# Ordering edges behind the side work of a hybrid S5/HGRN2 block, S5 parameters made in the first feed-forward part, the S5 scan placed in the heads, and ring quarters exchanged

## The chip, the cores and the metric

One core of one Trainium2 chip runs the kernel in one launch. The metric is device time in microseconds. Five engines work beside each other, each with its own in-order queue: TensorE (PE, with its weight loads PEld), VectorE (DVE), ScalarE (ACT), GpSimd (POOL), and SyncE (SP), which here issues nearly all DMAs.

## The reference, cut to what matters

All data is float32, 1024 tokens of width 1024.

```
h = x
h += 0.5 * swiglu(rmsnorm(h), gate, up, down)          # ffn1, hidden width 2816
u = rmsnorm(h);  s5_in, q, f, i, g, ga, gb = split(u @ w_in)
y_s5 = S5 scan of s5_in: states x_t = lam_bar * x_(t-1) + B_bar u_t (32 groups x 64 complex
       states), y = Re(C x) + D u;   lam_bar = exp(lam * dt), from the parameters alone
y_a  = (gelu(y_s5) @ glu_val) * sigmoid(gelu(y_s5) @ glu_gate)
o    = HGRN2 over 8 heads of 128 (gated linear recurrence), head norm, * silu(g)
h += (sigmoid(ga) * y_a + sigmoid(gb) * (o @ hg_w_out)) @ w_merge_out
h += 0.5 * swiglu(rmsnorm(h), ...)                     # ffn2
h += sigmoid(rmsnorm(h) @ ple_gate) * (p @ ple_proj);  out = rmsnorm(h)
```

## The kernel before, in words

Every large product is made on PE from pairs of rounded float32 parts: an operand is split by `split` or `piece` into hi (an ACT copy, L330 or L98) and lo (a subtraction on DVE or POOL, L331 or L99), and `mm3` issues three matmuls for each pair (L339). Weights come by DMA (L80) into two raw buffers and are split into 7 slots of a ring; a slot is refilled as soon as a product gives it back.

**FFN.** Hidden blocks f = 0 to 3 (`plain`) are multiplied directly, blocks 4 to 21 (`strassen`) by seven products of quarter size, of some 19 us for a block. The seven operands of the token side (A11, A22, A12 and the sums S1 to S4, made by `operands`) lie in seven "quarters" q0 to q6 of SBUF, four of which hold the normed input itself until block 3 is done. While blocks 5 to 21 run, 15 "jobs" prepare the down product: each loads 1 MB of the down weights (L578; the last four load x instead, L583) into a room of `r1`, makes four differences on DVE (L587) and stores them to DRAM (L600). The activations go to DRAM too (`gave`, L501). The down product (L707) then reads both back through rings in q4 and q5 (L612, L620) and splits each block on the way (`ready`).

**Side work.** Two lists, `queue` and `scan`, hold functions and waits. `tick` is called every few matmuls of the main products; it takes one element of each list: an integer n is a wait of n ticks, a function traces its instructions. `flush` and `scanned` empty a list at once. The framework orders the instructions of each engine itself: one that is traced later can be put ahead of one traced earlier, if the framework's planner holds it ready first.

**Mixer.** After the S5 input product (4 units) come the gates gg, ga, gb in `pair` form (again seven products, which begin with `flush("a11")`), then the eight HGRN2 heads (`hg_q`, `hg_f`, `hg_v`, with `hg_steps` in `queue`: seven levels of matmuls L1179, masked copies L1185 and multiplications L1191, L1192, then `kt`, `state`, `outp`, `back`), the S5 output product (glu), and the merge. `refill`, in the last gb pair, brings the normed input back into q0 for the heads. The S5 work is in `scan` from the first gg pair on: `lower_bound` and `s5_params` (225 small DVE instructions, L736 to L862, and two Sin on ACT, L812), then `s5_mats` for 8 blocks, then two turns of the scan proper (`turn`), each of 29 calls of `madd` with eight DVE instructions (L990 to L997), with matmuls and copies around them. A turn is 115 ticks long by its list. The scan works in `r1`; heads that end before it does spill their output (L1278).

Of the kernel before, what the change touches and what calls it, by code (L numbers as in the profile page):

```python
# [11 lines left out]
P = 128  # L12
# [38 lines left out]
class Weights:  # L51
# [23 lines left out]
    def fetch(self):  # L75
        while self.fetched < len(self.items) and len(self.items[self.fetched][1]) <= self.raw_free:
# [135 lines left out]
class Block:  # L212
# [58 lines left out]
    def tick(self):  # L271

        for q in (self.queue, self.scan):
# [144 lines left out]
    def operands(self, gain, roles=(0, 1, 2, 3, 4, 5, 6)):  # L418
# [18 lines left out]
        def sums(k):  # L437
# [3 lines left out]
            self.split(self.quarter(S1, k), s1, g)  # L441
# [5 lines left out]
        def plain(q, j, h):  # L447
            self.split(self.quarter(q, j % 4), scaled(j, h), (v, g)[j % 2])

# [7 lines left out]
        def chain(work, gap=0):  # L457
# [5 lines left out]
            sums=chain(sums, 4 if gain else 0),  # L463
# [21 lines left out]
    def ffn(self, name, gain, source, each, late=None):  # L485
# [30 lines left out]
        def plain(f):  # L516
            for h in range(2):
# [55 lines left out]
        def jobs():  # L573

            def load(n):
                room = self.r1[:, 4 * (n % 4):4 * (n % 4) + 4, :]
# [24 lines left out]
            begin(0)  # L601
            begin(1)
            for n in range(NP + 4):
                yield [lambda n=n: begin(n + 2), 2] + [x for i in range(4) for x in (lambda n=n, i=i: work(n, i), 3)] + [
                    lambda n=n: end(n)]
# [75 lines left out]
        ops = self.operands(gain)  # L681
# [19 lines left out]
        for n, (i, p) in enumerate(steps):  # L701
# [9 lines left out]
            for s in parts.pop(n):  # L711
                w.give(s)
            if n + 4 > len(steps):
                w.limit = None
# [38 lines left out]
    def lower_bound(self, p):  # L753
# [6 lines left out]
        nc.sync.dma_start(out=raw, in_=self.io["hg_lower_bound"])  # L760
        m = p.tile([P, HEADS], F32, name="lbm")
# [8 lines left out]
        v.tensor_scalar(out=self.lb1, in0=self.lb, scalar1=-1.0, scalar2=1.0, op0=ALU.mult, op1=ALU.add)  # L770

# [12 lines left out]

    def s5_params(self, pool):
# [8 lines left out]
        nc.sync.dma_start(out=a, in_=io["s5_log_dt"])  # L794
        self.sgn = c.tile([P, 1], F32, name="sgn")
        v.memset(self.sgn, 1.0)
        v.memset(self.sgn[64:128, :], -1.0)
        self.exp_small(pool, dt, a, SH, "s5x")
        er, sn, cs = (tl("s5" + n) for n in ("er", "sn", "cs"))
        v.tensor_tensor(out=a, in0=lre, in1=dt, op=ALU.mult)  # L800
        self.exp_small(pool, er, a, SH, "s5y")
        v.tensor_tensor(out=a, in0=lim, in1=dt, op=ALU.mult)
# [11 lines left out]
        self.pwr = pool.tile([P, G, T5 + 1], F32, name="s5pwr")  # L814
        self.pwi = pool.tile([P, G, T5 + 1], F32, name="s5pwi")
# [9 lines left out]
        self.rvr = pool.tile([P, G, T5], F32, name="s5rvr")  # L825
        self.rvi = pool.tile([P, G, T5], F32, name="s5rvi")
# [3 lines left out]
        yield  # L830

        wr, wi = tl("s5wr"), tl("s5wi")
# [13 lines left out]
        v.tensor_tensor(out=d, in0=d, in1=sc, op=ALU.mult)  # L846
        v.tensor_tensor(out=a, in0=a, in1=d, op=ALU.mult)
# [4 lines left out]
        self.wr = wr  # L852
        self.wis = tl("s5wis")
        v.tensor_scalar(out=self.wis, in0=wi, scalar1=self.sgn[:, 0:1], scalar2=None, op0=ALU.mult)

        self.chr = c.tile([P, 9, G // 2], F32, name="chr")
        self.chi = c.tile([P, 9, G // 2], F32, name="chi")
        for dst, src in ((self.chr, self.pre[T5]), (self.chi, self.pim[T5])):
# [3 lines left out]
        for i in range(2, 9):  # L862
            k, m = i // 2, i - i // 2
            self.cmul(pool, self.chr[:, i, :], self.chi[:, i, :], self.chr[:, k, :], self.chi[:, k, :],
                      self.chr[:, m, :], self.chi[:, m, :], [P, G // 2])
        self.d5 = c.tile([GH, G], F32, name="d5")
        nc.sync.dma_start(out=self.d5, in_=io["s5_d"])
        self.qd = self.dram.tile([8, P, 4, P], F32, name="s5q")
        self.pd = self.dram.tile([8, P, 4, P], F32, name="s5p")
        self.kd = self.dram.tile([GH, G, P], F32, name="s5k")  # L870
# [70 lines left out]
    def s5_steps(self):  # L941
# [12 lines left out]
        r4 = xr.rearrange("p g (a i) -> p g a i", i=NS)  # L954
        i4 = xi.rearrange("p g (a i) -> p g a i", i=NS)
        xs = pool.tile([P, RG, NCH], F32)
        u2 = pool.tile([P, RG, NCH], F32)
        prod = [pool.tile([P, GP * SC], F32) for _ in range(4)]
# [4 lines left out]
        steps = [lambda: self.lower_bound(early), 8]  # L963
        params = self.s5_params(early)
# [15 lines left out]
        def madd(dre, dim, sre, sim, lre, lim, shape):  # L980

            n = 1
# [3 lines left out]
            def view(x):  # L986
                x = x[:, 0:n]
                return x if len(shape) == 2 else x.rearrange("p (a b) -> p a b", b=shape[2])
            p1, p2, p3, p4 = (view(x) for x in prod)
            v.tensor_tensor(out=p1, in0=sre, in1=lre, op=ALU.mult)  # L990
            v.tensor_tensor(out=p2, in0=sim, in1=lim, op=ALU.mult)
            v.tensor_tensor(out=p3, in0=sim, in1=lre, op=ALU.mult)
            v.tensor_tensor(out=p4, in0=sre, in1=lim, op=ALU.mult)
            v.tensor_tensor(out=dre, in0=dre, in1=p1, op=ALU.add)
            v.tensor_tensor(out=dre, in0=dre, in1=p2, op=ALU.subtract)
            v.tensor_tensor(out=dim, in0=dim, in1=p3, op=ALU.add)
            v.tensor_tensor(out=dim, in0=dim, in1=p4, op=ALU.add)  # L997

        def turn(r):
# [35 lines left out]
            def local(i):  # L1035
                s = [P, GP, SC]
                bc = lambda x: x[:, 1, gp].unsqueeze(2).broadcast_to(s)
                madd(r4[:, :, :, i], i4[:, :, :, i], r4[:, :, :, i - 1], i4[:, :, :, i - 1],
                     bc(self.chr), bc(self.chi), s)
            for i in range(1, NS):  # L1040
                steps += [lambda i=i: local(i), 2]

            def carry(a0, a1):
                for a in range(a0, a1):
                    madd(r4[:, :, a, NS - 1], i4[:, :, a, NS - 1], r4[:, :, a - 1, NS - 1], i4[:, :, a - 1, NS - 1],
                         self.chr[:, NS, gp], self.chi[:, NS, gp], [P, GP])
            for a in range(1, SC, 2):
                steps += [lambda a=a: carry(a, min(SC, a + 2)), 2]

            def spread(i):  # L1050
                s = [P, GP, SC - 1]
# [715 lines left out]
```

## Time and profile before

| | |
|---|---|
| median of 3 runs | 2626.4 us (2623.2 to 2634.38) |
| the profiled execution, its own time | 2635.56 us |
| its span, first to last instruction | 2633.7 us |
| busy: PE, DVE, ACT, POOL | 2472.1, 1893.4, 914.0, 864.3 us |
| mean granted TensorE clock | 0.968 of full |

An engine's idle time is 2633.7 less its busy time. The granted clock is 1 at 2.4 GHz and 0.5 at 1.2 GHz; a stretch with a mean of 0.9 spent a fifth of its time at the lower level.

### The profile page before, as it was taken

The numbers are of one execution on the slowest core, as the hardware profiler recorded it, in microseconds if no ns is written. First come the engines' busy times: TensorE is split into PE (matmuls) and PEld (weight loads), VectorE is DVE, ScalarE is ACT, GpSimd is POOL, SyncE is SP. The second block draws the span as 40 slices with busy tenths as digits, with TensorE's granted clock in tenths as the row PEclk, the third lists the DMA queues.
The fourth block names the chain that finished last, engine by engine and source line by source line (L and its number), as shares of the span: only waits on it lengthen the run. The fifth ranks groups of instructions, "written<-read, shape, count | busy, mean of one in ns | idle before, by whom it ended". The sixth has DMA issues, their size and how long they took to land. (4 is left out here: it accounts for less than half of the span.)

```text
span 2633.7 us, 34224 instructions
## 1 busy us (share of the span) xinstructions
PE 2472.1 (94%) x12030; PEld 2067.5 (79%) x12030; DVE 1893.4 (72%) x3302; ACT 914.0 (35%) x1592; POOL 864.3 (33%) x602
## 2 busy tenths in 40 slices
PE   9999999999988998898999998989999999899997
PEld 7777778788866776787898887868877788688886
DVE  8898666658899678649545666946898766657756
ACT  4322232445443343231322223323322323345532
POOL 3254445100234544120211124552354444300143
PEclk9999999999998998899999999999999999899998
DMA  3478433867322345150231224452378432676313
GB/s 133 150 245 275 161 97 120 280 200 239 110 75 79 121 158 150 30 120 25 66 93 41 73 88 140 128 164 81 119 259 276 162 118 86 229 252 193 126 57 105
DMA packets 193932, 370.03 MB, mean 140 GB/s; under 512 B 34752, under 2 KB 49344, under 8 KB 193728
## 3 DMA queue, kind: packets, MB, share of 16 engines
q1 hardware_dynamic: 193072, 367.30, 42.7%
q8 instruction: 95, 1.56, 0.3%
q14 instruction: 77, 0.63, 0.1%
q10 hardware_dynamic: 688, 0.55, 0.1%
HBM read 255.84 MB, written 111.94 MB: 140 GB/s over the span
## 5 line engine op out<-in xcount | busy, mean ns | idle before, releaser
L339 PE MATMUL mm<-q,wsplit 128*128 128x512 f32 (+1 forms) x7452 | 1721.0, 391 | 89.0 <-ACT q L330 46.5
L339 PEld LDWEIGHTS mm<-q,wsplit 128*128 128x128 f32 x7452 | 1387.7, 191 | 390.8 <-ACT q L330 53.3
L99 POOL TENSOR_TENSOR wsplit<-wraw,wsplit 128x512 fp32r<-128x512 f32 x368 | 526.9, 1445 | 1162.6 <-ACT wsplit L98 470.8
L98 ACT ACTIVATE wsplit<-wraw 128x512 fp32r<-128x512 f32 x464 | 283.9, 625 | 520.4 <-DVE wraw L119 196.1
L707 PE MATMUL mm<-wsplit 128*128 128x512 f32 x1848 | 426.5, 394 | 14.7 <-ACT wsplit L330 13.7
L707 PEld LDWEIGHTS mm<-wsplit 128*128 128x128 f32 x1848 | 350.7, 190 | 90.2 <-ACT wsplit L330 14.5
L331 DVE TENSOR_TENSOR wsplit<-space,wsplit 128x512 fp32r<-128x512 f32 x308 | 208.4, 714 | 126.1 <-PE mm L707 93.3
L330 ACT ACTIVATE wsplit<-space 128x512 fp32r<-128x512 f32 x308 | 193.1, 631 | 212.4 <-PE mm L707 175.2
L119 DVE TENSOR_TENSOR wraw<-wraw 128x512 f32<-128x512 f32 x153 | 174.2, 1138 | 69.2 <-POOL wsplit L99 63.3
L99 POOL TENSOR_TENSOR wsplit<-t,wsplit 128x512 fp32r<-128x512 f32 x51 | 85.6, 1678 | 266.6 <-ACT wsplit L98 232.0
L534 DVE TENSOR_TENSOR t<-t,mm 128x512 f32<-128x512 f32 x252 | 166.2, 677 | 0.2
L1179 PE MATMUL mm<-space,space 128*128 128x128 f32 x896 | 114.1, 282 | 25.2 <-DVE space L1139 14.9
L1179 PEld LDWEIGHTS mm<-space,space 128*128 128x128 f32 x896 | 109.8, 197 | 31.3 <-DVE space L1139 15.8
L99 DVE TENSOR_TENSOR wsplit<-wraw,wsplit 128x512 fp32r<-128x512 f32 x96 | 85.3, 891 | 66.1 <-ACT wsplit L98 60.5
L1185 DVE COPY_PREDICATED space<-masks,mm 128x256 f32<-128x256 int32 x112 | 58.4, 521 | 90.6 <-PE mm L1179 90.5
L587 DVE TENSOR_TENSOR r<-r 128x512 f32<-128x512 f32 x120 | 104.5, 882 | 13.0 <-DMA r<-in_ffn_w_down_dram 6.1
L339 PE MATMUL mm<-wsplit,q 128*128 128x256 f32 x768 | 101.5, 288 | 0.0
L339 PEld LDWEIGHTS mm<-wsplit,q 128*128 128x128 f32 x768 | 95.2, 193 | 0.5 <-PE mm L1244 0.4
L98 ACT ACTIVATE wsplit<-t 128x512 fp32r<-128x512 f32 x51 | 32.3, 633 | 174.9 <-DVE t L119 156.7
L505 POOL TENSOR_TENSOR a<-a 128x512 f32<-128x512 f32 x44 | 66.4, 1508 | 64.9 <-DVE a L525 48.3
L1308 DVE TENSOR_TENSOR t<-t,mm 128x512 f32<-128x512 f32 x105 | 69.5, 677 | 19.2 <-ACT t L1311 9.3
L537 ACT ACTIVATE t<-t 128x512 f32<-128x512 f32 x72 | 45.5, 631 | 104.5 <-DVE t L534 104.5
(247 smaller groups left out, 2120.2 us busy)
## 6 DMA issues: line engine op xcount, KB each, us to landing
space<-ffn_act SPq DMA_DIRECT2D x154, 256.0 KB, 3.5
ffn_act<-a SPq DMA_DIRECT2D x110, 256.0 KB, 3.7
wraw<-in_ffn_w_gate_dram SPq DMA_DIRECT2D x44, 512.0 KB, 3.4
wraw<-in_ffn_w_up_dram SPq DMA_DIRECT2D x44, 512.0 KB, 5.0
r<-in_ffn_w_down_dram SPq DMA_DIRECT2D x22, 1024.0 KB, 6.4
ffn_sums<-r SPq DMA_DIRECT2D x22, 1024.0 KB, 8.8
wraw<-in_w_in_dram SPq DMA_DIRECT2D x44, 512.0 KB, 3.5
space<-ffn_sums SPq DMA_DIRECT2D x88, 256.0 KB, 2.7
```

The costliest lines, as they stand in the source:

```text
L98: self.nc.scalar.activation(hi, src, AF.Copy)
L99: engine.tensor_tensor(out=lo, in0=src, in1=hi.bitcast(F32), op=ALU.subtract)
L119: sub = lambda out, x, y: v.tensor_tensor(out=out, in0=x, in1=y, op=ALU.subtract)
L330: self.nc.scalar.activation(hi, src, AF.Copy)
L331: lo_engine.tensor_tensor(out=lo, in0=src, in1=hi.bitcast(F32), op=ALU.subtract)
L339: self.last = nc.tensor.matmul(ps, al if p == 2 else ah, bl if p == 1 else bh, start=p == order[0] and i == 0, stop=p == order[2] and i == ...
L505: g.tensor_tensor(out=x[n], in0=x[a], in1=x[b], op=op)
L534: add = lambda out, x, y: v.tensor_tensor(out=out, in0=x, in1=y, op=ALU.add)
L587: v.tensor_tensor(out=room[:, out, :], in0=room[:, x, :], in1=room[:, y, :], op=ALU.subtract)
L707: self.last = nc.tensor.matmul(ps[j], a[:, j * P:(j + 1) * P], b, start=p == 0 and m == 0, stop=p == NP - 1 and m == 2)
L1179: nc.tensor.matmul(ps[:, c * HC:(c + 1) * HC], K[:, cc], Q[:, cc], start=True, stop=True)
L1308: add = lambda o, x, y: nc.vector.tensor_tensor(out=o, in0=x, in1=y, op=ALU.add)
```

## The change

1. `paced`: every function taken by `tick` is traced inside it. Each instruction that it traces gets an ordering edge (without a semaphore) to the last instruction traced before it on the same engine, SP's DMAs included, so it can't be placed ahead of that one. `flush` and `scanned` don't use it. The first two job loads are traced in it too.
2. `fetch` stops at `limit`, so that raw weights of the next stage are not asked for before 16 steps are left of the down product's 77.
3. FFN operands: A11 is made early, in `sums`, and lies in q4; S1 is made late, by a new chain (`again`), in q0. The wait between `sums` is 10 ticks instead of 4.
4. Jobs use three rooms instead of four, and load after the store of the job before; the fourth room is the arena of the S5 parameters in ffn1 (`aside`), of which each job takes one of 13 parts (`go`).
5. The down product's rings are opened and loaded after the first two of the last block's seven products, and its first splits come after the 4th, 5th and 7th (before: loads after the 2nd and 4th, splits after the 6th and 7th).
6. `s5_params` ends by storing its result in DRAM (`s5_keep`), and `s5_steps` loads it again. The mixer's list then has the matrices alone (166 ticks, with waits of 9); both turns of the scan are put in `scan` after head 0's products.
7. `madd` treats real and imaginary part in one instruction of twice the length: four DVE instructions instead of eight.

```diff
     def fetch(self):
-        while self.fetched < len(self.items) and ...
+        while self.fetched < (self.limit or len(self.items)) and ...
@@ tick
-                    f()
+                    self.paced(f)
+    def paced(self, fn):
+        traced = self.nc.cur_bb.bb.instructions
+        n = len(traced)
+        prev = {}
+        for i in reversed(traced[max(0, n - 400):n]):
+            prev.setdefault(i.engine, i)
+        mark = traced[n - 1]
+        fn()
...
+        for i in traced[start:]:
+            if i.engine in prev:
+                self.tc.add_manual_dep(i, prev[i.engine].name, mybir.DependencyInfo(
+                    mybir.DependencyClass.NoSync, mybir.DependencyReason.DATA), reason="paced")
@@ operands
+            if early:
+                self.split(self.quarter(A11, k), x11, g)
+            else:
+                self.split(self.quarter(S1, k), s1, g)
+        def again(k):
+            s1 = self.t()
+            v.tensor_tensor(out=s1, in0=scaled(k, 0), in1=scaled(4 + k, 0), op=ALU.add)
+            self.split(self.quarter(S1, k), s1, g)
@@ ffn
-                    self.queue += ops["a11"] + ops["a22"]
+                    self.queue += ops["s1"] + ops["a22"]
-                room = self.r1[:, 4 * (n % 4):4 * (n % 4) + 4, :]
+                room = self.r1[:, 4 * (n % 3):4 * (n % 3) + 4, :]
-            begin(0)
-            begin(1)
+            self.paced(lambda: (begin(0), begin(1)))
+            other = aside(Arena(self.r1[:, 12:16, :].rearrange("p a b -> p (a b)"))) if aside else iter(())
+            go = lambda: next(other, None)
-                yield [lambda n=n: begin(n + 2), 2] + [x for i in range(4) for x in (lambda n=n, i=i: work(n, i), 3)] + [lambda n=n: end(n)]
+                do = [lambda n=n, i=i: work(n, i) for i in range(4)]
+                yield [do[0], 3, do[1], 2, go, 2, do[2], 3, do[3], 1, lambda n=n: end(n), 1, lambda n=n: begin(n + 2)]
-            if n == 1:
+            if n == 0:
+                ring["w"] = self.space(4, F32)
+            elif n == 1:
                 ring["s"] = self.space(5, F32)
                 for i in range(6):
+                    load_w(i)
                     load_s(i)
             elif n == 2 and late:
                 late()
-            elif n == 3:
-                ring["w"] = self.space(4, F32)
-                for i in range(6):
-                    load_w(i)
-            elif n == 5:
-                ready(0)
-                ready(1)
-            elif n == 6:
-                ready(2)
+            elif n in (3, 4, 6):
+                ready((3, 4, 6).index(n))
-        ops = self.operands(gain)
+        ops = self.operands(gain, roles=(4, 1, 2, 3, 0, 5, 6), early=True, gap=10)
+            if n + 16 == len(steps):
+                w.limit = None
+                w.fetch()
@@ s5_params: 12 yields between its parts, result packed in one tile
+        self.s5_keep = self.dram.tile([P, n], F32, name="s5keep")
+        nc.sync.dma_start(out=self.s5_keep, in_=keep)
@@ s5_steps
-        steps = [lambda: self.lower_bound(early), 8]
-        for wait in (20, 9, 16):
-            steps += [go(params), wait]
-        steps += [go(part[0]), 2, go(part[0]), 14]
+        first = [kept, go(part[0]), 6]
         for b in range(8):
-            if b < 7:
-                steps += [go(part[b + 1]), 2, go(part[b + 1]), 4]
-            steps += [go(part[b]), 2]
+            first += [go(part[b]), 9, go(part[b])]
+            first += [go(part[b + 1]), 9] if b < 7 else []
-        def madd(dre, dim, sre, sim, lre, lim, shape):
+        def madd(d, s, i, gp):
...
+            v.tensor_tensor(out=p1, in0=s, in1=re, op=ALU.mult)
+            v.tensor_tensor(out=p2, in0=s[:, ::-1], in1=im, op=ALU.mult)
+            v.tensor_tensor(out=d, in0=d, in1=p1, op=ALU.add)
+            v.tensor_tensor(out=d, in0=d, in1=p2, op=ALU.add)
-        return steps + turn(0) + turn(1) + [self.s5_done]
+        return first, turn(0) + turn(1) + [self.s5_done]
@@ mixer
-        scan = self.s5_steps()
+        scan, later = self.s5_steps()
             self.queue += self.hg_steps(j)
+            if j == 0:
+                self.scanned()
+                self.scan = later
@@ tile_block
-    b.ffn("ffn1", ..., finish("mix_norm", True, (2, 3)))
+    b.ffn("ffn1", ..., finish("mix_norm", True, (2, 3)), aside=b.s5_params)
```

## Rows read from the trace of the kernel before

**Rows 1.** The page's first part: busy time, share of the span, instructions.
```profile
span 2633.7 us, 34224 instructions
...
PE 2472.1 (94%) x12030; PEld 2067.5 (79%) x12030; DVE 1893.4 (72%) x3302; ACT 914.0 (35%) x1592; POOL 864.3 (33%) x602
```

**Rows 2.** Waits of PE, whole span: us in total, times, longest us.
```profile
PE mm L339 <- ACT q L330: 46.5, 15, 10.3
PE mm L339 <- ACT wsplit L98: 31.7, 14, 8.7
```

**Rows 3.** Windows: length, busy us (instructions) of each engine, granted clock, DMA.
```profile
130.00:150.00 20.00, 15.19 (x56) 11.84 (x55) 20.00 (x28) 7.02 (x12) 13.42 (x6) 0.83 0.49 169
240.00:275.00 35.00, 29.51 (x121) 23.29 (x120) 28.82 (x36) 8.50 (x15) 19.05 (x13) 0.95 0.88 304
475.00:495.00 20.00, 15.14 (x56) 11.99 (x55) 12.62 (x18) 7.65 (x13) 4.91 (x3) 0.83 0.89 300
770.00:800.00 30.00, 19.55 (x66) 13.54 (x65) 29.76 (x102) 13.51 (x23) 9.00 (x8) 0.77 0.18 60
815.00:865.00 50.00, 35.72 (x140) 28.42 (x140) 47.46 (x148) 14.37 (x30) 24.09 (x18) 0.83 0.24 77
...
1030.00:1060.00 30.00, 17.93 (x61) 13.26 (x60) 29.53 (x141) 8.49 (x15) 8.54 (x6) 0.72 0.33 114
1060.00:1090.00 30.00, 20.09 (x104) 17.82 (x103) 23.84 (x81) 10.06 (x23) 5.61 (x5) 0.77 0.11 36
1170.00:1250.00 80.00, 67.64 (x488) 62.06 (x486) 75.62 (x306) 12.49 (x27) 8.75 (x4) 0.98 0.11 34
1300.00:1400.00 100.00, 98.84 (x710) 91.46 (x709) 49.71 (x111) 26.18 (x44) 13.16 (x10) 1.00 0.26 77
...
2025.00:2045.00 20.00, 14.74 (x53) 11.34 (x52) 16.06 (x22) 4.55 (x8) 8.11 (x6) 0.83 0.77 281
2265.00:2290.00 25.00, 15.14 (x52) 11.42 (x51) 16.44 (x18) 9.83 (x17) 10.78 (x7) 0.73 0.74 267
```

**Rows 4.** SP's waits, 455 to 480.
```profile
SPq L80 <- DVE wsplit L99: 14.5, 1, 14.5
```

**Rows 5.** SP's timeline, 456 to 482: start, us, line, out<-in, count.
```profile
475.34 3.76 SPq L612 DMA_DIRECT2D space<-ffn_act  x7
```

**Rows 6.** ACT's timeline, 768 to 784.
```profile
776.48 1.28 ACT L812 ACT_TABLE_LOAD   x1
781.54 0.23 ACT L812 ACTIVATE r<-r 128x32 f32<-128x32 f32 x1 [3.78 <-DVE r L811]
```

**Rows 7.** DVE groups by line, 750 to 842: busy us, mean ns.
```profile
L781 DVE TENSOR_TENSOR r<-r 128x32 f32<-128x32 f32 x8 | 3.9, 486 | 0.0
...
L743 DVE TENSOR_TENSOR r<-r 128x32 f32<-128x32 f32 (+1 forms) x18 | 2.8, 180 | 0.1
```

**Rows 8.** Windows of line L587 alone: length, DVE busy us, clock, DMA.
```profile
200.00:300.00 100.00, 23.62 (x28) 0.98 0.72 249
300.00:400.00 100.00, 0.00 (x0) 1.00 0.35 108
```

**Rows 9.** Windows before and after 290, engines as in rows 3.
```profile
100.00:290.00 190.00, 179.70 (x769) 146.75 (x768) 163.50 (x203) 56.17 (x97) 89.70 (x58) 0.97 0.72 251
290.00:470.00 180.00, 177.92 (x781) 146.18 (x780) 113.67 (x141) 54.38 (x93) 92.16 (x67) 1.00 0.32 101
```

**Rows 10.** DVE groups by shape, 990 to 1100 (first turn of the scan).
```profile
L994 DVE TENSOR_TENSOR r<-r 128x128 f32<-128x128 f32 x7 | 4.9, 702 | 0.0
```

**Rows 11.** The same, 1100 to 1260 (second turn).
```profile
L997 DVE TENSOR_TENSOR r<-r 128x128 f32<-128x128 f32 x7 | 2.7, 388 | 0.0
...
L991 DVE TENSOR_TENSOR r<-r,chi 128x8 f32<-128x8 f32 x15 | 2.4, 162 | 0.0
```

**Rows 12.** DVE's timeline in a head after the scan, 1302 to 1318.
```profile
1307.56 0.45 DVE L1185 COPY_PREDICATED space<-masks,mm 128x256 f32<-128x256 int32 x1 [2.00 <-PE mm L1179]
```

**Rows 13.** Waits of DVE, whole span.
```profile
DVE space L1136 <- ACT t L1135: 35.2, 8, 8.6
```

More of the change, by code (lines that the diff above doesn't have):

```diff
@@ L75, in fetch @@
     def fetch(self):
-        while self.fetched < len(self.items) and len(self.items[self.fetched][1]) <= self.raw_free:
+        while self.fetched < (self.limit or len(self.items)) and len(self.items[self.fetched][1]) <= self.raw_free:
             raws = []
@@ L280, in tick @@
                 if not isinstance(f, str):
-                    f()
+                    self.paced(f)
[7 more added lines that the diff above has]
+        fn()
+        traced = self.nc.cur_bb.bb.instructions
+        start = next(k for k in reversed(range(len(traced))) if traced[k] is mark) + 1
+        for i in traced[start:]:
+            if i.engine in prev:
+                self.tc.add_manual_dep(i, prev[i.engine].name, mybir.DependencyInfo(
+                    mybir.DependencyClass.NoSync, mybir.DependencyReason.DATA), reason="paced")
     def after(self, n, fn):
@@ L416, in ffn_plan, with operands @@
         self.planned = {**getattr(self, "planned", {}), name: len(self.w.items)}
-    def operands(self, gain, roles=(0, 1, 2, 3, 4, 5, 6)):
+    def operands(self, gain, roles=(0, 1, 2, 3, 4, 5, 6), early=False, gap=4):
         v = self.nc.vector
@@ L462, in operands @@
         return dict(
-            sums=chain(sums, 4 if gain else 0),
+            sums=chain(sums, gap if gain else 0),
+            s1=chain(again) + ["s1"],
             a11=chain(lambda k: plain(A11, k, 1)) + ["a11"],
@@ L483, in product, with ffn @@
         return ps
-    def ffn(self, name, gain, source, each, late=None):
+    def ffn(self, name, gain, source, each, late=None, aside=None):
         nc, w = self.nc, self.w
@@ L783, in cmul, with s5_kept @@
         v.tensor_tensor(out=oim, in0=oim, in1=t, op=ALU.add)
+    def s5_kept(self, keep):
+        n = G * (T5 + 1)
+        m = G * T5
+        three = lambda x: x.rearrange("p (g i) -> p g i", g=G)
+        self.pwr, self.pwi = three(keep[:, 0:n]), three(keep[:, n:2 * n])
+        self.rvr, self.rvi = three(keep[:, 2 * n:2 * n + m]), three(keep[:, 2 * n + m:2 * n + 2 * m])
+        self.wr, self.wis = (keep[:, 2 * n + 2 * m + i * G:2 * n + 2 * m + (i + 1) * G] for i in range(2))
     def s5_params(self, pool):
@@ L794, in s5_params @@
         nc.sync.dma_start(out=a, in_=io["s5_log_dt"])
+        self.d5 = c.tile([GH, G], F32, name="d5")
+        nc.sync.dma_start(out=self.d5, in_=io["s5_d"])
+        bounds = self.lower_bound(pool)
+        next(bounds)
         self.sgn = c.tile([P, 1], F32, name="sgn")
@@ L797, in s5_params @@
         v.memset(self.sgn[64:128, :], -1.0)
+        yield
+        yield from bounds
         self.exp_small(pool, dt, a, SH, "s5x")
+        yield
         er, sn, cs = (tl("s5" + n) for n in ("er", "sn", "cs"))
@@ L978, in fetch @@
             return m
-        def madd(dre, dim, sre, sim, lre, lim, shape):
+        def madd(d, s, i, gp):
+            shape = list(d.shape)
             n = 1
@@ L987, in view, with over @@
                 x = x[:, 0:n]
[L988 to L997, printed above, removed]
+                return x.rearrange("p (t g) -> p t g", t=2) if len(shape) == 3 else x.rearrange(
+                    "p (t g a) -> p t g a", t=2, g=GP)
+            def over(x):
+                return x if len(shape) == 3 else x.unsqueeze(3).broadcast_to(shape)
+            re = over(self.chr[:, i, gp].unsqueeze(1).broadcast_to([P, 2, GP]))
+            im = over(self.chj[:, i, :, gp])
+            p1, p2 = (view(x) for x in prod)
+            v.tensor_tensor(out=p1, in0=s, in1=re, op=ALU.mult)
+            v.tensor_tensor(out=p2, in0=s[:, ::-1], in1=im, op=ALU.mult)
+            v.tensor_tensor(out=d, in0=d, in1=p1, op=ALU.add)
+            v.tensor_tensor(out=d, in0=d, in1=p2, op=ALU.add)
         def turn(r):
```

76 lines of the change are left out of this document (35 added, 41 removed).

## Prediction

> **What bounds the kernel now.** I read the page's first part first: PE is busy 2472.1 of 2633.7 us, so it is the bound, and it idles 161.6 us [rows 1]. With the mean granted clock of 0.968, 3.2% of the span, 84 us, is lost to the lower clock level. Some 246 us at most are there to be won, and the question is which of them the change touches.
>
> Next the waits of PE. The largest are on side results: 46.5 us on ACT's split L330 and 31.7 us on the weight split L98, in pieces of up to 10 us [rows 2]. They are lumps, not a steady lack, so I then looked at windows around the lumps [rows 3]. For each I count the loss as length less PE busy, plus length times (1 less the clock): every stall is followed by a stretch at the lower of the two levels, and that stretch costs nearly as much again. (It counts a little too much, as part of the idle time lies in the lower level too.) The reader should see ten lumps: 130:150 loses 4.81 + 3.4 = 8.2; 240:275 7.2; 475:495 8.3; 770:800 10.45 + 6.9 = 17.4; 815:865 22.8; 1030:1060 20.5; 1060:1090 16.8; 1170:1250 14.0; 2025:2045 8.7; 2265:2290 16.6. That is 140 us. By contrast 1300:1400, heads without a scan, loses 1.2.
>
> What stands behind each lump? At 475 the down product starts. SP stood 14.5 us at L80 for a raw buffer of the next stage's weights [rows 4], and only then issued L612 and, behind it, L620, at 475.34 [rows 5]; the product's first splits wait for these. At 770 ACT loads a table at 776.48 and then runs Sin (L812) after a wait of 3.78 us for DVE [rows 6], with an operand's split queued behind it; DVE is 29.76 of 30 us busy with S5 parameters. At 815 DVE is still on them (47.46 of 50). At 1030 and 1060 DVE is busy 29.53 and 23.84 of 30 us, with the scan's first turn (29 calls of eight instructions) beside `refill`. At 240 and 2025 the DMA share is 0.88 and 0.77: the job loads and the weight loads collide.
>
> **The change part by part.** Gains first.
>
> *Down starts* (edits 2 and 5): the raw weights stop in front of L612, and the rings fill two products earlier. What is late next are the first three splits, now one at a time between the last block's products, so two or three products of PE work cover them. The two lumps hold 24.9; I take 23.
>
> *S5 parameters* (edits 4 and 6): 225 small DVE instructions leave the mixer. Their means lie from 180 ns to 486 ns [rows 7]; at 0.18 they are 41 us of DVE, at 0.486 109. The lumps at 770 and 815 hold 40.2. The matrices (`s5_mats`) and their DMAs stay there, so I take 32, not all. The new store and the load of the result (one DMA each) lie behind nothing that PE waits for.
>
> *Jobs* (edits 1 and 4): L587 issues 28 instructions, 23.62 us, between 200 and 300, and none after that [rows 8]: 0.84 us each, 51 us for the 60. They are traced for blocks 5 to 19, so the planner puts them all early. Held by edges they spread over 15 blocks of 19 us. Each job's 1 MB load then goes out every 19 us, and weight loads are no longer late at 240 and 2025: 15.9 us there, taken 13.
>
> *Operands* (edit 3): A11 is there early, and S1 comes by the chain that A11 had. The lump at 130 is 8.2; I assume the same in the second feed-forward part, 16.4. The late chain stays, with one more addition per block, so I take 5.
>
> *Scan* (edits 6 and 7): its first turn leaves 1030:1090, where 37.3 are lost. `refill` itself stays, so 30. Its second turn leaves 1170:1250: 12 of 14.0.
>
> Together 23 + 32 + 13 + 5 + 30 + 12 = 115.
>
> Now costs. *DVE in ffn1.* From 290 to 470, without jobs, DVE is busy 113.67 of 180 us, from 100 to 290 163.50 of 190 [rows 9]. Less the jobs' 51 that makes 226 of 370, 61%. Jobs over 15 blocks (285 us) add 18%, parameters of 41 us 14%: 93%, against 86% in the busy 190 us before. The cover is thin: what is over comes out as waits of PE. Below, nothing, if the parts fit in the gaps; above, parameters slowed as the scan's L994 was, 702 ns in the first turn [rows 10] against 388 for its like L997 in the second [rows 11], a factor of 1.81: 41 becomes 74, load 105%, 5% of 285 = 14 over. To this come Sin among Silu: up to four table loads of 1.28 us. I take 8, bounds 0 and 14 + 5 = 19.
>
> On that factor: the Trainium skill's page SBUF — State Buffer, section Who interferes with whom, says that a DVE instruction with two SBUF inputs contends with a GpSimd instruction that reads SBUF. POOL is half busy here, 92.16 of 180 us, and 13.16 of 100 in the heads, so the rule speaks against moving parameters into ffn1 and for moving the scan into heads; by it the upper bound would be the value, and the sum 11 us smaller. On the table: the page ScalarE: Activation LUTs, section What ACT_TABLE_LOAD costs, gives 1.28 us of load and 1.38 us of drain for a switch. The row agrees on 1.28; with its drain four switches would be 10.6 us of ACT, an estimate, not 5.1.
>
> *Scan in the heads.* A turn is now 14 calls on 256 elements and 15 on 16, four instructions each. A 128x256 instruction of DVE takes 0.45 us [rows 12], a short one 0.162: 56 x 0.45 + 60 x 0.162 = 34.9 a turn, against 112 x 0.388 + 120 x 0.162 = 62.9 before. In 1170:1250 the second turn's 62.9 us cost PE 14.0, or 0.22 for each us. Two turns at that rate: 69.8 x 0.22 = 16 (rounded). Below, nothing: beside a head without scan DVE stands 2.00 us in each level for L1179, room for a call's four. Above, times 1.81: 28. I take 16. By its waits the list is 230 ticks long, and 231 are left between head 0 and head 7's q, so little is emptied at once.
>
> *Waits taken in order* (edit 1): an instruction with an edge can't be overtaken by what was traced before it, and it in turn holds up nothing but side work that comes after. But where a side instruction waits for another engine, DVE stands. The nearest row is L1136, standing behind its ACT copy L1135: 35.2 us in 8 times [rows 13], of which PE felt a part. Bounds 0 and 35; I take 12, a third, since the side work's waits are mostly on DMAs issued a block earlier.
>
> Costs 8 + 16 + 12 = 36. Net 79 less. The profiled execution took 2635.56, which is 9.2 above the median of the runs shown; its lumps are taken to be those of the median too. 2635.56 - 79 = 2556.6 by the profile, 2547 at the median.
>
> **The rivals.** *The stalls come back at the next wait.* PE leaves a lump and meets, earlier than now, the next late weight or operand: DMA is at 0.72 over 100:290, and DVE at 93% in ffn1. For it: the lumps have different releasers one behind another (L330 and L98 in the same stretches). Against: the windows between lumps (1300:1400, or 290:470 with 177.92 of 180) run full. Half the gains then, 58, less 36: 22, so 2604.
>
> *The edges don't bind.* They hold only on an engine that had an instruction among the last 400 traced, and order nothing among engines; DMAs could go early as now. Then jobs (13), operands (5) and the edges' cost (12) vanish: 115 - 18 - 24 = 73, so 2553. It can't be told from the forecast by time, only by where L587 lies.
>
> *Slower: the scan beside each level.* DVE feeds every level of a head: L1179 waits for L1185 to L1192, 56 levels in all. A call of four instructions, 1.8 us, traced ahead of L1185 now stays ahead of it. If all 69.8 us of it went on PE's path and the clock fell after each as at 1060:1090 (6.9 for 9.91 idle), the heads would cost 69.8 x 1.7 = 119 in place of 16. The rest of the sum is 115 - 20 = 95: from 95 on the change gains nothing, from 108 on it is slower by the bound below, and at 119 it gives 2626 + 24 = 2650. For it: heads are serial by level. Against: the 2.00 us stand of DVE, and the 0.22 of 1170:1250.
>
> *It does nothing*: each lump moves elsewhere whole; 2626.
>
> **How the numbers follow.** 0.5%, 13 us, is about what a measurement of this kernel can tell from no change. The forecast has 0.70, its own range 2485 to 2604: at best nearly all of the lumps' 148.7 (with the second 8.2) less 8 without costs, at worst half of the gains with middling costs, which is also the first rival's point. The first rival has 0.16: 0.12 of it faster by the bound, 0.04 within it. The edges not binding, 0.05, faster. The scan on the path 0.05, all slower. Nothing won 0.04, of which 0.03 same and 0.01 slower. Faster: 0.70 + 0.12 + 0.05 = 0.87; same 0.07; slower 0.06. The range 2485 to 2604 leaves out the slower rival, the last one, and half of the first: 0.17; the upper bounds of all costs at once (19 + 28 + 35 = 82, net 33, 2593) lie within it.
>
> **What would show it right or wrong.** Right: L812 and its two Sin between 160 and 400 us; L587 in all windows up to 450 in ffn1; no L80 ahead of L612 and no idle of PE at the down starts; no scan before 1060, and PE as full at 770 to 1090 as at 290 to 470; DVE above 90% in ffn1 with PE still near 98%; waits of L1179 in the heads of some 10 to 30 us more than in 1300:1400; the clock near 1. Wrong: new lumps in ffn1 on L98 or L330, where a part of the parameters stands ahead of a split; a clock in the heads below 0.95; or a weight wait right after each place where one was taken away.

## The result, and the profile after

The kernel became slower: 2661.5 us at the median of 4 runs (2659.2 to 2667.7) against 2628.9 (2623.2 to 2634.4), ratio 1.0128, 95% interval 1.0098 to 1.0158. The forecast was 2547, with a range of 2485 to 2604.

The changed kernel's page, first part, and its waits of PE over the whole span (us in total, times, longest):

```profile
span 2665.6 us, 33892 instructions
...
PE 2485.9 (93%) x12030; PEld 2072.1 (78%) x12030; DVE 1902.8 (71%) x3079; ACT 905.9 (34%) x1586; POOL 856.6 (32%) x602
```
```profile
PE mm L355 <- ACT wsplit L98: 50.9, 27, 3.7
PE mm L355 <- ACT q L346: 42.9, 14, 10.1
PE mm L956 <- DVE r L951: 13.8, 6, 9.6
```

Against [rows 1, 2] the waits on a weight's split (L98) have gone from 31.7 us in 14 pieces of up to 8.7 to 50.9 in 27 of up to 3.7: the lumps became a steady lack. Its place shows in the windows (columns as in rows 3), above all against [rows 9]:

```profile
100.00:290.00 190.00, 175.78 (x743) 143.13 (x742) 168.69 (x306) 55.94 (x97) 81.99 (x54) 0.96 0.47 161
290.00:470.00 180.00, 157.75 (x663) 126.65 (x662) 146.84 (x247) 48.27 (x96) 80.49 (x56) 0.97 0.52 179
...
800.00:870.00 70.00, 53.71 (x211) 41.40 (x210) 51.58 (x75) 25.04 (x44) 37.38 (x27) 0.85 0.30 103
...
1040.00:1070.00 30.00, 30.00 (x135) 24.87 (x134) 12.37 (x17) 12.60 (x22) 14.89 (x11) 1.00 0.42 141
...
1300.00:1400.00 100.00, 89.29 (x600) 80.42 (x599) 81.51 (x211) 18.47 (x37) 13.24 (x10) 0.97 0.14 49
1640.00:1670.00 30.00, 25.77 (x84) 19.21 (x84) 30.00 (x33) 12.60 (x23) 19.43 (x13) 0.78 0.52 175
...
2000.00:2230.00 230.00, 213.84 (x895) 171.22 (x894) 172.13 (x202) 62.45 (x107) 107.85 (x76) 0.97 0.53 184
```

From 290 to 470 PE lost 2.1 us before and 22.3 now, and 16.2 from 2000 to 2230. Refill (1040:1070) is full, as forecast.

Both kernels issue 12030 matmuls, in an order that is the same at the level of stages, so the start of the n-th in one trace less its start in the other shows where time goes. The places are given by the time in the kernel before; positive is lost. (Each trace is one execution. Two traces of one and the same kernel, the best run below and its repeat, agree within 0.1 us in the feed-forward parts, and differ by 1.2 from 722 to 895 and by 3.3 at the first down start.)

```
start to 158        -3.4     1023 to 1549 (refill, heads)  -23.1
158 to 475 (ffn1)  +33.8     1549 to 1735 (merge)           +8.2
475 to 517 (down)   -3.1     1735 to 1948                   +2.0
517 to 722           0.0     1948 to 2235 (ffn2)           +17.9
722 to 895         -12.3     2235 to 2317 (down)            -1.0
895 to 1023         +8.2     2317 to 2615                   +3.4
```

The sum is 30.5. Nearly all the loss lies in the Strassen blocks of the two feed-forward parts. One block of ffn1, first SP's timeline (start, us):

```profile
375.73 0.33 SPq L527 DMA_DIRECT2D ffn_act<-a  x1
391.02 0.37 SPq L626 DMA_DIRECT2D ffn_sums<-r  x1
391.44 3.26 SPq L609 DMA_DIRECT2D r<-in_x_dram  x4
396.23 0.33 SPq L80 DMA_DIRECT2D wraw<-in_ffn_w_gate_dram  x1
399.05 0.33 SPq L80 DMA_DIRECT2D wraw<-in_ffn_w_up_dram  x1
```

SP stands 15 us at a job's store (L626), which waits for the job's last difference (L613) on DVE; then it issues the load of a later job, and only then, after another 1.5 us for the raw buffer, the next block's weights. (The last four jobs load x in four DMAs, L609, as here; the others load down weights in one, L604.) SP's waits, 290 to 470:

```profile
SPq L626 <- DVE r L613: 77.5, 7, 15.0
```

In [rows 4] SP also stood, but for a raw buffer, which is the weights' own pace. And DVE in the same block (start, us):

```profile
381.46 2.53 DVE L119 TENSOR_TENSOR wraw<-wraw 128x512 f32<-128x512 f32 x2
383.91 0.16 DVE L909 COPY chr<-r 64x16 f32<-64x16 f32 x1
...
386.13 1.27 DVE L810 TENSOR_TENSOR r<-chj,chr 128x16 f32<-128x16 f32 x1
387.32 0.16 DVE L807 TENSOR_TENSOR chr<-chr,r 128x16 f32<-128x16 f32 x1
387.41 0.68 DVE L613 TENSOR_TENSOR r<-r 128x512 f32<-128x512 f32 x1
...
390.31 0.68 DVE L613 TENSOR_TENSOR r<-r 128x512 f32<-128x512 f32 x1
390.92 0.68 DVE L119 TENSOR_TENSOR wraw<-wraw 128x512 f32<-128x512 f32 x1
```

Between the third and the fourth difference of the weights (L119) lie 7 us of parameters, products' sums and job differences. ACT's split waits for the fourth (6.46 us, until 391.69), and the raw buffer is free only after it. So there were two suspects: SP's order (theory 1) and the parameters on DVE (theory 2).

### The profile page after: what moved, and what is told of

It reads as the page before. It is cut to its first block, busy times and chain, and to the rows that moved or that the text cites. A ratio compares the mean times of both kernels' runs of the same rounds, so it can differ in the third digit from the quotient of the medians.

```text
span 2665.6 us, 33892 instructions
## 1 busy us (share of the span) xinstructions
PE 2485.9 (93%) x12030; PEld 2072.1 (78%) x12030; DVE 1902.8 (71%) x3079; ACT 905.9 (34%) x1586; POOL 856.6 (32%) x602
## 5 line engine op out<-in xcount | busy, mean ns | idle before, releaser
L355 PE MATMUL mm<-q,wsplit 128*128 128x512 f32 (+1 forms) x7452 | 1734.2, 393 | 101.0 <-ACT wsplit L98 50.9
L98 ACT ACTIVATE wsplit<-wraw 128x512 fp32r<-128x512 f32 x464 | 283.1, 626 | 603.0 <-DVE wraw L119 202.4
L119 DVE TENSOR_TENSOR wraw<-wraw 128x512 f32<-128x512 f32 x153 | 176.2, 1152 | 54.9 <-POOL wsplit L99 50.4
L99 POOL TENSOR_TENSOR wsplit<-t,wsplit 128x512 fp32r<-128x512 f32 x51 | 74.2, 1455 | 335.7 <-ACT wsplit L98 324.2
L99 DVE TENSOR_TENSOR wsplit<-wraw,wsplit 128x512 fp32r<-128x512 f32 x96 | 79.3, 833 | 91.6 <-ACT wsplit L98 82.5
L1219 PE MATMUL mm<-space,space 128*128 128x128 f32 x896 | 114.3, 282 | 22.8 <-DVE space L1179 11.4
L613 DVE TENSOR_TENSOR r<-r 128x512 f32<-128x512 f32 x120 | 123.0, 1025 | 0.2 <-DMA r<-in_ffn_w_down_dram 0.2
L98 ACT ACTIVATE wsplit<-t 128x512 fp32r<-128x512 f32 x51 | 32.3, 632 | 189.3 <-DVE t L119 136.2
```

Source lines behind the costliest of these rows:

```text
L98: self.nc.scalar.activation(hi, src, AF.Copy)
L99: engine.tensor_tensor(out=lo, in0=src, in1=hi.bitcast(F32), op=ALU.subtract)
L119: sub = lambda out, x, y: v.tensor_tensor(out=out, in0=x, in1=y, op=ALU.subtract)
L355: self.last = nc.tensor.matmul(ps, al if p == 2 else ah, bl if p == 1 else bh, start=p == order[0] and i == 0, stop=p == order[2] and i == ...
L613: v.tensor_tensor(out=room[:, out, :], in0=room[:, x, :], in1=room[:, y, :], op=ALU.subtract)
L1219: nc.tensor.matmul(ps[:, c * HC:(c + 1) * HC], K[:, cc], Q[:, cc], start=True, stop=True)
```

## The experiments

Ratios are to the kernel before on the same chip, whose median lay between 2625 and 2636 us in the four groups of runs. "Drift" is the difference of starts as in the table above: "ffn1" is the drift from 158 to 441, "ffn2" from 1948 to 2235; the changed kernel has +31.2 and +17.9.

**Late store.** The job list ends `do[3], 1, begin(n + 2)`, and `end(n - 1)` stands after `do[1]`.
```diff
-yield [do[0], 3, do[1], 2, go, 2, do[2], 3, do[3], 1, lambda n=n: end(n), 1, lambda n=n: begin(n + 2)]
+yield [do[0], 3, do[1], 1] + ([lambda n=n: end(n - 1)] if n else []) + [1, go, 2, do[2], 3, do[3], 1] + (
+        [lambda n=n: end(n)] if n == NP + 3 else []) + [1, lambda n=n: begin(n + 2)]
```


> The changed kernel (2661.5 us at the median), with each job's store traced one job later, in the middle of the next job, when its four differences have long been made; edges, parameters and scan stay as they are. Theory 1: the feed-forward parts got slower because SP, in order, stands up to 15 us at a job's store (L626, waiting for the job's last difference L613 on DVE) with the next block's raw weights (L80) behind it. Then SP's wait at L626 falls from 90.7 us between 150 and 470 to under 15, PE's waits on L98 in 290:470 fall from 22.2 to under 8, and the time falls by 25 to 40, to 2622 to 2637. Theory 2: DVE is full in ffn1 (146.8 of 180 us in 290:470) and the weights' differences L119 stand behind side work; then DVE's order is hardly changed and the time stays within 10 of 2661.


2627.1 us, 0.9969 (0.9957 to 0.9981): theory 1's time, won in ffn2 (+17.9 became -11.8). SP's wait at L626 fell to 9.4 us, as theory 1 had it. But PE's waits on L98 from 290 to 470 fell only to 15.1, not below 8, and ffn1 stayed at +26.3, which theory 1 did not say.

**No edges.** `self.paced(f)` in `tick` is `f()`.


> The changed kernel without the ordering edges: what tick takes is traced without them, all else is left. Theory 1 (SP stands at the job stores because the edges hold them in the middle of the weights' loads): the jobs are put early again, in bursts, the steady loss of 18 to 27 us in each feed-forward part goes, and single collisions of 7 to 9 us come back: 2630 to 2645. Theory 2 (DVE full with the parameters in ffn1): edges or not, DVE has the same work in ffn1; ffn1 keeps its loss of 27, ffn2 has none to lose: 2640 to 2661.


2622.8 us, 0.9953 (0.9937 to 0.9969), better than either theory had it: ffn1 +16.3, ffn2 +2.1.

**The kernel before with edges alone.** `paced` is added and used by `tick` and by the first two loads.


> The kernel before (2628.9 us), with the ordering edges alone added. Theory 1 (edges put the jobs' stores in the midst of the weights' loads): both feed-forward parts lose 10 to 25 us each, less what the bursts at 240 and 2025 cost (16): 2640 to 2660. Theory 2 (DVE full with parameters in ffn1): there are no parameters in ffn1, so the edges spread the jobs and gain: 2610 to 2630.


2614.0 us, 0.9918 (0.9901 to 0.9935). Theory 1 missed: the edges by themselves gain, 11.4 in ffn1 and 14.3 in ffn2. Yet SP stands there at the store too (150 to 470):

```profile
SPq L616 <- DVE r L603: 127.4, 15, 11.1
```

So standing is not the harm. What follows the store differs; SP of this kernel:

```profile
350.93 0.37 SPq L616 DMA_DIRECT2D ffn_sums<-r  x1
356.07 0.33 SPq L80 DMA_DIRECT2D wraw<-in_ffn_w_gate_dram  x1
358.88 0.33 SPq L80 DMA_DIRECT2D wraw<-in_ffn_w_up_dram  x1
359.26 1.85 SPq L599 DMA_DIRECT2D r<-in_x_dram  x4
```

After the store SP still has 4.7 us to wait for the raw buffer, and the loads come behind the weights.

**Parameters in the mixer.** `aside` is dropped; the list begins with the 13 parts, 3 ticks apart.


> The changed kernel with the S5 parameters made at the start of the mixer's list again (13 parts, 3 ticks apart), not in ffn1; all else is left. Theory 1 (SP at the job stores): ffn1 loses nearly as much as ffn2 does without parameters, 18 in place of 27 to 30, and the mixer loses some 20 about 770 to 860: 2660 to 2680. Theory 2 (DVE full): ffn1's loss goes, 25 us, and the mixer's 20 come back: 2650 to 2660, and PE's waits on L98 in 290:470 fall below 8.


2674.6 us, 1.0148 (1.0130 to 1.0166); ffn1 +22.1, ffn2 +15.9. With the jobs as they are, the parameters make 9 us in ffn1; theory 1.

**Load moved.** The store stays; the next load goes a few ticks into the next job.
```diff
+yield [do[0], 3] + ([lambda n=n: begin(n + 1)] if n else []) + [do[1], 2, go, 2, do[2], 3, do[3], 1, lambda n=n: end(n), 1]
```


> The changed kernel (2661.5) with the job's store where it is and the next job's load moved away from behind it, to a few ticks into the next job (and so one job ahead instead of two). Theory 1a: what hurts is that SP waits for the last difference at all, with the weights behind; then nothing changes, 2652 to 2665. Theory 1b: SP's wait alone is covered (the kernel before with edges waits 127 us there and loses nothing); the weights are late because the job's load goes out between the store and them: four issues of 3.5 us and 1 MB more ahead of them in the DMA queues. Then most of the 34 us of the run with the late store is won: 2630 to 2642.


2623.0 us, 0.9983 (0.9972 to 0.9993): theory 1b, with 7 us more than it had. The three rooms are left as changed, so they are not the cause. Its window 2000:2230, to be read against the one above:

```profile
2000.00:2230.00 230.00, 230.00 (x1017) 190.44 (x1016) 182.81 (x229) 70.31 (x120) 128.17 (x84) 1.00 0.62 210
```

PE has no idle time left, though SP waits at L626 for 95.4 us in it. ffn1 still loses 26.6.

**Late store and parameters in the mixer.**


> The run with the late store (2627) with the S5 parameters back in the mixer. Theory 1 alone: the parameters cost ffn1 some 7 us and save the mixer 21, so 2636 to 2645. With theory 2 for what is left (ffn1 still loses 16 to 20 with the late store, since DVE is full there with jobs and parameters): ffn1 gains 20 or more, the mixer loses 21: 2620 to 2630.


2610.8 us, 0.9934 (0.9915 to 0.9953): better than both theories had it; ffn1 goes from +26.3 to -10.1.

**Jobs as before, parameters in the mixer.**


> The changed kernel with the jobs as before (four rooms, load first, then four differences, then the store) and the parameters in the mixer; edges, rings, operands and scan as changed. Theory 1 (edges are good, the new order of a job's steps is bad): both feed-forward parts as in the kernel before with edges, 20 less each than before; refill and the heads as changed, 20 less; the mixer's start 10 more: 2629 - 50 = 2579, 2570 to 2595. Rival: the changed rings, operands or the scan take back what the edges give: 2605 to 2630.


2603.9 us, 0.9909 (0.9892 to 0.9925), the same as the kernel before with edges alone. The feed-forward parts came as theory 1 had it (-11.4, -14.3); the 2579 counted on 20 in each and found 6 to 9 less, and the mixer's start (+8.8) and the merge took back some of what refill gave.

**Eight instructions in madd**, on the late store.


> The run with the late store (2627) with the scan's madd in eight instructions of half the length again. If each us of the scan's DVE time costs the heads 0.22 us, as was reckoned: 56 us more DVE, 12 us more time, 2636 to 2642. If the heads cover it: 2624 to 2631.


2625.1 us, 0.9987 (0.9974 to 0.9999) against 0.9969: next to nothing. DVE's busy time from 1070 to 1550 is 325.0 against 313.2 us, so the pairing saves 12 us there, not 56: the durations of single instructions, which the 56 adds up, overlap one another (in the block above one of 0.16 us starts at 387.32 and the next at 387.41).

**Part first.** As the run with the load moved, with `go, 2` ahead of `do[0]`.


> The run with the load moved (2623) with the parameters' part put at the head of each job, ahead of its first difference, some 5 ticks earlier; the amount of DVE work stays. Theory 2a, place: the parts hurt because they stand in DVE's queue ahead of the weights' fourth difference (L119), whose split frees the raw buffer for the next load; moved away, most of ffn1's 16 to 20 us come back: 2600 to 2613. Theory 2b, amount: DVE has no room for 70 to 77 us of parameters wherever they stand: 2617 to 2630.


2642.1 us, 1.0064 (1.0041 to 1.0086): worse. The differences moved too, by two ticks, and ffn2, which has no parts, went from -14.3 to +8.7. It tells nothing of the parts, but much of how tight the jobs' place is.

**Load moved and parameters in the mixer.**


> The run with the load moved (2623) with the parameters in the mixer. With both causes gone (the job's load ahead of the weights, the parameters in ffn1) both feed-forward parts gain 16 to 20 against the kernel before, the mixer's start loses 8: 2598 to 2608, and no window in 290:470 where PE waits for L98. If only one of the two was a cause, not under 2612.


2596.9 us, 0.9894 (0.9871 to 0.9918); ffn1 -11.4, ffn2 -14.3. Both were causes.

**The same, next stage's weights held.** `self.paced(w.fetch)` where the limit is lifted.


> The same, with the raw weights of the next stage fetched with an ordering edge too. In the changed kernel they are traced late, but SP still issues two of them (L80) ahead of the down product's first L648 and L640. If that is why the down starts won only 3 to 4 of the 23 us reckoned: PE's waits on L346 at both down starts fall below 1.5 us and the time by 4 to 12 against the run beside it. If the rings are late by themselves, no change (within 3).


2597.8 us, 0.9889 (0.9859 to 0.9919): no difference that can be told. The order is now as meant (L648 ahead of L80), PE is full from 470 to 500, but the second down start still has a wait of 3.6 us.

**The same, scan behind the matrices.** Both turns follow the mixer's list.


> The same as the run with load moved and parameters in the mixer, with both turns of the scan right behind the matrices in the mixer's list, as before, and not in the heads. Reckoned: 30 + 12 in refill and head 2, less 16 in the heads, 26; by the drift of the traces 20. So 15 to 28 more than the run beside it. If the heads pay back all of it: within 5.


2600.9 us, 0.9908 (0.9885 to 0.9930). The list had become so long that the first turn moved by 40 us only; it can't decide.

**Part last**, and **part without edges**, both on the run with the load moved.
```diff
+yield [do[0], 3] + ([lambda n=n: begin(n + 1)] if n else []) + [do[1], 4, do[2], 3, do[3], 1, lambda n=n: end(n), go, 1]
```
```diff
-                    self.paced(f)
+                    f() if getattr(f, "free", False) else self.paced(f)
...
+            go.free = True
```


> The run with the load moved (2623) with the parameters' part traced after the job's store in place of between its second and third difference; differences, store and load stand one tick from where they were, so the second feed-forward part, which has no parts, is the control. Theory 2a, place: at its old place a part lies on DVE between the weights' third and fourth difference (L119 at 376.6 and 383.7), and the raw buffer comes free late; at the new place ffn1 gains 10 or more against the run with the load moved (where it lost 16 from its start to the down product), ffn2 stays within 3: 2605 to 2615. Theory 2b, amount: ffn1 loses 13 to 20 as there: 2618 to 2628.

> The run with the load moved (2623) with the parameters' parts traced without ordering edges, jobs and all else with them. Theory 2a, place in DVE's order: the planner now puts the parts where DVE is free and early; ffn1 gains 5 to 15: 2608 to 2618. Theory 2b, amount: no gain, ffn1 loses 13 to 20 all the same, perhaps in one lump about 160 to 240, where the run without any edges lost 13: 2618 to 2630.


Part last: 2630.5 us, 1.0000 (0.9983 to 1.0017): by its time theory 2b; ffn1 +17.0 in place of +26.6, ffn2 -11.3. Its trace is of its fastest execution (2621.8 of 2621.8 to 2636.3), so these two may be too good. Part without edges: 2603.9 us, 0.9907 (0.9883 to 0.9931), somewhat more than theory 2a had; ffn1 +5.4, ffn2 -14.3. Its window, to be read against the changed kernel's 290:470:

```profile
290.00:470.00 180.00, 178.42 (x785) 146.75 (x784) 141.49 (x171) 53.20 (x91) 95.10 (x66) 1.00 0.57 195
```

The parts now run at 119 to 232, cost 14 in one lump there, and half of it comes back before 300. Their durations add up to about what they do in the part-last run (54 us of DVE in both), and ffn1 is 12 us better: with the amount alike, that much is order. Held a little in every block, they lengthen every block. In the run with the load moved they add up to 77 us, so its distance to these two is order and amount together.

**Scan early.** As the best run, with waits of 1 and 5 ticks in the mixer's list and the scan right behind it.


> The best run (load moved, parameters in the mixer; 2597, ratio 0.9894) with the mixer's list made tighter and the scan right behind it, so that its first turn lies at about 1000 to 1080, beside the last gate and refill, as in the kernel before. If moving the scan is worth what was reckoned (30 + 12 - 16 = 26), 2615 to 2628, with PE's lumps at 1030 to 1090 back. If refill's lumps came from side work put ahead of it, which the edges cure, and not from the scan: 2594 to 2606.


2640.1 us, 1.0045 (1.0024 to 1.0066). The time is above that of the first theory, and most of the loss is none that it named: 44 us are lost from 807 to 959, where PE stands at L956 behind the tightened matrices:

```profile
PE mm L956 <- DVE r L951: 56.4, 4, 44.9
```

But the lumps of refill are back, as that theory had it. The stretch that [rows 3] show at 1030 lies 29 us later here, and PE is busy 21.82 of 30 us in place of 17.93:

```profile
1059.00:1089.00 30.00, 21.82 (x81) 16.70 (x80) 29.36 (x47) 8.03 (x14) 12.58 (x9) 0.83 0.37 127
```

From 1023 to 1123 this run gains 4.3 on the kernel before, and the best run 25.8. The heads take most of that back: to 1549 it is 12.0 against 16.9, so here the scan's move is worth some 5 us in sum.

**The best run again.**


> The best run once more, beside the three others on the same chip: ratio 0.987 to 0.992 to the kernel before, 2590 to 2605.


2604.3 us, 0.9906 (0.9884 to 0.9927). It beats both kernels: 1% under the one before, 2.2% under the changed one (0.9906 / 1.0128). From the kernel before with edges alone (0.9918) it can't be told apart. Its blocks are full:

```profile
290.00:470.00 180.00, 179.69 (x793) 148.53 (x792) 139.37 (x175) 56.20 (x96) 93.36 (x63) 1.00 0.63 212
```

## Why the prediction was wrong

Two causes, of which either alone is enough in ffn1; ffn2, which never has parameters, shows the first by itself:

```
ffn1 / ffn2                 parameters in ffn1    parameters in the mixer
load ahead of weights         +31.2 / +17.9          +22.1 / +15.9
load behind weights           +26.6 / -14.3          -11.4 / -14.3
```

**Waits taken in order: the step that failed.** It said that an instruction with an edge "in turn holds up nothing but side work that comes after", and priced edges by DVE's worst wait, at 12. SP's queue is in order as well, and what came after on it were the next block's weights. The jobs' DVE time was counted; their stores and loads, and what stands behind these on SP, were put at nothing, without a reason. The jobs' new order of steps, in which the load follows the store at once, costs 64 us where the parameters are not in ffn1 (22.1 + 11.4 and 15.9 + 14.3), and 37 where they are (31.2 - 26.6 and 17.9 + 14.3). That the load, and not the wait at the store, is what makes the weights late is shown by the run with the load moved.

How the load does it the traces show too. In the second feed-forward part, in 9 of 13 blocks of the changed kernel SP still stood 1.3 to 3.6 us for the raw buffer after it had issued the load, so issuing it first delayed nothing there. But the gate weights landed late. From issue to landing they took, in the 13 to 15 blocks from 1955 to 2230 (us, least, median, most), in the changed kernel, in the run with the load moved and in the run with the late store:

```profile
DMA to landing us min/median/max: 5.2/5.8/6.9
DMA to landing us min/median/max: 3.2/3.4/4.3
DMA to landing us min/median/max: 3.1/3.3/3.8
```

In the run with the late store the loads go out ahead of the weights as well, but there SP waited 4.3 to 14.5 us between a load and the weights, and they landed on time. So the edges and the new order sent each load out just ahead of the weights, which landed 2.4 us later for it. Over 13 blocks that makes 31 us, an estimate from these medians; 32.2 were found in ffn2 (17.9 + 14.3).

**DVE in ffn1: mis-sized.** Reckoned at 8 with bounds 0 and 19, measured 38 with good jobs (26.6 + 11.4), 9 with the jobs as changed. The load was judged by its sum, 93%, and PE was to stay near 98%; DVE was in fact 85% busy in the changed kernel (168.7 + 146.8 of 370) and 87% in the run with the load moved (166.6 + 155.1), and PE 90% and 91%. The prediction's own sign of being wrong came: waits on L98 with a part of the parameters ahead of a split. An instruction held in the midst of a chain (weights, difference, split, buffer free, next weights) lengthens the chain. The part-without-edges run gives back 21 of the 38, of which 12 are order with the amount alike. The part-last run gives back 10, perhaps because its parts are short (54 us in place of 77); that, and how much of the last 17 is room, stays open. The 41 us of parameters took the least of the means quoted; in the kernel before their durations add up to 57.8.

**Jobs: right, and better than reckoned** once both are away: 11.4 + 14.3 = 26 in place of 13, by the edges alone. The second rival, edges that don't bind, is out: the jobs' differences are 13.75 us from 200 to 300 and 17.49 from 300 to 400 in the changed kernel, against 23.62 and nothing [rows 8].

**Down starts: 23 reckoned, 4 measured.** The kernel before with edges alone, without these edits, wins 16 there (7.2 + 8.9), so no run shows that the edits themselves gain. The limit moves the place where L80 is traced, not where SP has it. SP of the changed kernel:

```profile
501.96 2.24 SPq L80 DMA_DIRECT2D wraw<-in_w_in_dram  x2
504.41 1.70 SPq L527 DMA_DIRECT2D ffn_act<-a  x2
506.20 1.51 SPq L648 DMA_DIRECT2D space<-in_ffn_w_down_dram  x3
```

The first L648 goes out at 506.2, behind the two L80, and PE starts on the down product at 513.8; in the kernel before, L612 went out at 475.34 [rows 5] and PE started at 485.5. Putting it in order gained nothing that can be told.

**Parameters out of the mixer: 32 reckoned, 4 measured.** The lumps were read as the parameters' own, but of DVE's 29.76 us from 770 to 800 they took 13.6, and of the 47.46 from 815 to 865 14.4. 12.3 were won up to 895 and 8.2 given back: the matrices, traced with an edge on PE too, make PE stand at L956 for 13.8 us in 6 pieces. The run without edges has no such wait and wins 17.3 from 722 to 1023, and the kernel before with edges alone loses 16.1 there: in the mixer's start the edges cost some 13 to 16. No run drops them there alone. The run with the parameters in the mixer loses 10.5 from 722 to 1023, so the move is worth 15 there, less than the 38 that it costs with good jobs.

**Scan: right in sum, in part by luck.** 42 less 16 reckoned, 23.1 measured: about 32 won to the first head, 9.3 lost in the heads; two misses that cancel. The first is the move's doing: the run without edges wins 32.6 up to 1123 as well, the kernel before with edges alone 10.0. In the heads the edges help: without them 23.3 are given back. From 1023 to 1549 the kernel before with edges alone wins 8.5, the run without edges 9.3, the changed kernel, with both, 23.1, and the best run 16.9. The pairing saved 12 us of DVE, not 56, of which the time shows nothing. The rival with the scan on PE's path (119) is refuted by those 9.3.

**Operands**: 5 reckoned, 1.4 measured (start to 158, and 1735 to 1948); but the kernel before with edges alone wins 1.9 at the start too, so no gain of the edit is shown. **Not foreseen**: 8.2 in the merge, which the kernel before with edges loses too (8.9) and the run without edges by half (3.8), at a place where DVE is busy 30.00 of 30 us; the cause was not looked for. The first rival, stalls that come back at the next wait, came nearest, but let them halve the gains; here the change itself made the weights late.

The way of counting lumps said that every stall costs nearly as much again in clock. In 1170:1250 it is 1.6 by the clock for 12.36 idle, in 240:275 1.75 for 5.49 [rows 3]; the sum took them as they are.

## What to carry to other kernels

When side work is pinned into program order, go through each in-order queue that it touches, the DMA-issuing one first: a store that waits, with a load right behind it, holds that load back until just ahead of what the main work issues next there, which then lands late. Put the main work's DMA between the store and the load, or the load well ahead. And judge side work on an engine that is part of a producer's chain not by the engine's busy share alone, but also by whether it stands between two links of the chain; a single lump can cost less than a little in every block.

## What was unexpected in the hardware

Sin on ACT needed no table load in ffn1: the changed kernel has none between 25.8 and 786.3, though both Sin (L857) run there, at 250.9 and 254.7, each 0.23 us, among Silu. The four loads reckoned, 5.1 us or 10.6, didn't come; 15 loads in the program became 9; four of the six that went stood around the two Sin of the mixer, the other two in the heads. Nor does a load cost more than its 1.28 us there: in the kernel before an activation ends at 800.77, the load runs from 800.79 to 802.07, and the next activation starts at 802.08.

Small DVE instructions beside POOL took over seven times as long. In the run with the load moved, a copy of 64x16 takes 1.26 us while POOL splits, and 0.17 when it doesn't:

```profile
377.23 1.26 DVE L909 COPY chr<-r 64x16 f32<-64x16 f32 x1
378.50 1.24 DVE L910 COPY chr<-r 64x16 f32<-64x16 f32 x1
379.77 1.22 DVE L909 COPY chj<-r 64x16 f32<-64x16 f32 x1
381.00 0.17 DVE L910 COPY chj<-r 64x16 f32<-64x16 f32 x1
```
```profile
376.90 1.57 POOL L99 TENSOR_TENSOR wsplit<-t,wsplit 128x512 fp32r<-128x512 f32 x1 [4.53 <-ACT wsplit L98]
378.43 2.53 POOL L99 TENSOR_TENSOR wsplit<-wraw,wsplit 128x512 fp32r<-128x512 f32 x2
```

The Trainium skill's page SBUF — State Buffer, section Who interferes with whom, says that copies can enter a mode that contends with GpSimd, where whoever issues first holds the shared ports for the whole instruction. These rows agree: each of the three long copies ends as a POOL split ends; the mode itself no row shows. In sum the durations of the parameters' instructions are 69.6 us in the changed kernel and 77.2 in the run with the load moved, against 57.8 before.
